# Windowed attention with four adjacent output rows per partition, the value product in two column tiles, and the last unit in one store

## The chip, the cores and the metric

The kernel runs on one core of a Trainium2 chip. The metric is the device time in microseconds (us) of one execution. The span of a profile is some 1.8 us shorter than the time of the same execution (before: 940.6 us and 942.39 us).

## The reference, cut to what matters

```python
B, S, D, W = 4, 4096, 1536, 64              # float32 in and out
q_w, k_w, v_w = (x.reshape(B, S // W, W, D) for x in (q, k, v))
logits = einsum('bnwd,bnud->bnwu', q_w, k_w) * D ** -0.5
attn   = softmax(logits)                    # over the 64 keys of the window
out    = einsum('bnwu,bnud->bnwd', attn, v_w).reshape(B, S, D)
```

There are 16384 rows; each window of 64 rows attends only to itself. The program reads 302 MB and writes 101 MB, and computes little.

## The kernel before

It works through 32 units of 512 rows. GpSimd issues all loads but the first of q (cast to fp16 on the way, two units ahead, two landing buffers per tensor) and all stores but the last, and copies each landed tensor into the working buffer. TensorE transposes q and k, forms logits, and multiplies the exponentials with v; VectorE and ScalarE copy transposes and scale the output by the reciprocal of the row sums.

```python
# [cut] P=128 partitions, SLOTS=4 rows per partition and unit, R=2, H=2, NO=3 output buffers
def rows(x, row0, n, r):     # r adjacent rows lie in one partition
    return x[row0 : row0 + P * n].rearrange("(h p r) d -> p h (r d)", p=P, r=r)

def store(u):                # two adjacent rows: 256 runs of 12288 B
    nc.gpsimd.dma_start(
        out=rows(of, u * UR, SLOTS, R), in_=slots(outs[u % NO], 0, SLOTS, R)
    ).then_inc(d_o[u % NO], 16)

def hand_over(x, u, dst, m, g):
    gp.wait_ge(landed[x][u % NL], 16 * ((u + u % NL) // NL))
    gp.wait_ge(m, u)
    gp.tensor_copy(out=dst..., in_=landing[x][u % NL]...).then_inc(c_l, 1)
    # [cut: wait for the copy, tell TensorE]
    request(x, u + NL)       # the load of two units later

# TensorE, value product: one weight set for all 128 output rows of a row slot
for h in range(H):
    for t, r, what in ((1,0,"s"), (1,1,"s"), (0,0,"sv"), (0,1,"sv"), (1,0,"v"), (1,1,"v")):
        n = R * h + t
        w = ets[h][:, r, t, :]                       # 128 x 128
        ld = nc.tensor.ldweights(w)
        # [cut] "s": the row sums; "v": three matmuls of 512 columns of v16[:, R*h + r, :]

# GpSimd's loop
for u in range(1, N):
    hand_over("q", u, q16, m_q, g_q)
    hand_over("k", u, k16, m_k, g_k)
    gp.wait_ge(m_q, u + 1)
    store(u - 1)
    hand_over("v", u, v16, m_v, g_v)

# SyncE, the last unit in two stores
for h, c in enumerate((1, 3)):
    for a in range(2):
        sy.wait_ge(n_e[a], c)
    sy.dma_start(out=rows(of, base + R*P*h, R, R), in_=slots(o, R*h, R*h + R, R)).then_inc(d_l[h], 16)
```

The softmax here doesn't subtract the row's maximum and nothing guards it: scores larger than these inputs give would overflow.

## Time and profile before

| | before |
|---|---|
| time, median of the first 3 runs | 942.81 us (942.58 to 943.32) |
| span of the profiled run | 940.6 us |
| late unit | 29.17 us |
| early unit, inputs prefetched | 20.4 us |
| granted TensorE clock | 0.86 |

The slices of the page show the busy share of each engine in tenths. A full DMA row beside a TensorE row of 6 to 8 says that transfers bound the kernel. The lines are in the prediction.

The trace has one record for every DMA packet (start, duration, bytes, queue), without the number of the DMA engine that carried it. Each DMA ends with one 4-byte completion packet on each of the 16 engines. Sorting the 16 completion packets of one DMA gives when the first engine and the last engine were done with it; the difference is called the **spread**. One engine is followed by taking, at the end of a packet, the packet that starts there; where several start together this can slip, so such chains are used only where one engine is clearly apart from the others.

### The profile page before, as it was taken

The page shows a single profiled execution, that of the slowest core. Times are in us where ns is not written, and L with a number is a line of the kernel's source. Part 1 is how long each engine was busy: PE and PEld are TensorE (multiplying, and loading weights), DVE is VectorE, ACT ScalarE, POOL GpSimd, SP SyncE. Part 2 cuts the span into 40 slices and gives each one's busy share as a digit, 9 for nine tenths or more (in the row PEclk, how much of TensorE's full clock was granted, in tenths as well). Part 3 has the DMA queues.
Part 4 walks back from the last instruction along what each step waited for, and adds up shares of the span by engine and source line. Part 5 has one row for each costly group of instructions (what it writes and reads, how often), then busy time and mean ns, then how long its engine had stood idle before and what let it go on. Part 6 is the DMA issues. An engine that isn't in the chain of part 4 may idle for free. (4 is left out here: it accounts for less than half of the span.)

```text
span 940.6 us, 11415 instructions
## 1 busy us (share of the span) xinstructions
PE 656.9 (70%) x4096; PEld 397.2 (42%) x3456; DVE 279.9 (30%) x453; ACT 335.6 (36%) x642; POOL 341.0 (36%) x225
## 2 busy tenths in 40 slices
PE   0888676866777768677676676776867768677673
PEld 0555344533445434454244443445433445334450
DVE  0344322333313333133331333321333223332231
ACT  0444433333333333332432324332334333343332
POOL 4244333344333443333423334233343333433221
PEclk9999978889878788888887978887789788888887
DMA  9999999999999999999999999999999999999998
GB/s 258 218 217 274 259 241 283 283 280 268 233 283 283 279 276 230 277 284 279 281 232 271 283 280 283 238 263 283 280 282 247 253 283 281 282 255 245 283 297 367
DMA packets 26652, 253.35 MB, mean 269 GB/s; under 512 B 2064, under 2 KB 2064, under 8 KB 10256
## 3 DMA queue, kind: packets, MB, share of 16 engines
q0 software_dynamic: 26208, 246.95, 100.0%
q1 hardware_dynamic: 432, 6.29, 1.6%
q14 instruction: 10, 0.08, 0.0%
q8 instruction: 2, 0.03, 0.0%
HBM read 301.99 MB, written 100.66 MB: 428 GB/s over the span
## 5 line engine op out<-in xcount | busy, mean ns | idle before, releaser
L155 PE MATMUL lt<-xq,xk 128*128 128x256 f16 x1536 | 215.5, 292 | 0.0
L143 PE MATMUL tp<-ident,k 128*128 128x128 f32 x768 | 146.9, 335 | 82.9 <-PEq L209 71.7
L292 POOL COPY v<-vl 128x3072 f32<-128x3072 f32 x31 | 85.1, 2744 | 287.4 <-DMA vl<-in_v_dram 287.4
L155 PEld LDWEIGHTS lt<-xq,xk 128*128 128x128 f16 x1536 | 159.5, 104 | 32.8
L143 PE MATMUL tp<-ident,q 128*128 128x128 f32 x768 | 113.9, 297 | 75.4 <-PEq L209 39.3
L143 PEld LDWEIGHTS tp<-ident,k 128*128 128x128 f32 x768 | 113.9, 174 | 102.8 <-issue 100.2
L218 ACT COPY xk<-tp 128x512 f32<-128x512 f32 x96 | 59.3, 618 | 260.1 <-ACTq L209 260.1
L184 PEld LDWEIGHTS <-et 128*128 128x128 f16 x384 | 34.6, 108 | 277.9 <-issue 272.2
L143 PEld LDWEIGHTS tp<-ident,q 128*128 128x128 f32 x768 | 92.7, 152 | 115.9 <-issue 115.2
L218 DVE COPY xk<-tp 128x512 f32<-128x512 f32 x96 | 66.5, 693 | 225.9 <-DVEq L209 225.9
L292 POOL COPY k<-kl 128x3072 f32<-128x3072 f32 x31 | 85.3, 2750 | 109.2 <-DMA kl<-in_k_dram 109.2
L292 POOL COPY q<-ql 128x3072 f32<-128x3072 f32 x31 | 85.1, 2744 | 106.3 <-DMA ql<-in_q_dram 106.3
L111 PE MATMUL o<-v,et 128*128 128x512 f16 x384 | 114.4, 443 | 0.0
L218 ACT COPY xq<-tp 128x512 f32<-128x512 f32 x96 | 59.7, 622 | 130.9 <-ACTq L209 130.9
L260 ACT ACTIVATE et<-lt,zeros 32x128 f16<-32x128 f32 x256 | 92.1, 360 | 39.3 <-ACTq L209 36.1
L111 PE MATMUL sp<-ones,et 128*128 128x1 f16 x256 | 25.6, 169 | 112.3 <-PEq L209 110.0
L247 DVE TENSOR_SCALAR out<-o,rs 128x512 f32<-128x512 f32 x128 | 91.1, 747 | 34.1 <-DVEq L209 29.9
L218 DVE COPY xq<-tp 128x512 f32<-128x512 f32 x96 | 66.2, 690 | 97.8 <-DVEq L209 97.6
L271 ACT ACTIVATE out<-tp,rs 128x512 f32<-128x512 f32 x64 | 44.0, 688 | 134.6 <-ACTq L209 104.4
L111 PE MATMUL tp<-v,et 128*128 128x512 f16 x256 | 91.1, 443 | 0.0
L237 DVE RECIPROCAL rs<-sp 128x2 f32<-128x2 f32 x64 | 10.7, 168 | 259.5 <-DVEq L209 259.3
L111 PE MATMUL lt<-v,et 128*128 128x512 f16 x128 | 57.6, 450 | 0.0
(21 smaller groups left out, 224.5 us busy)
## 6 DMA issues: line engine op xcount, KB each, us to landing
out_dram<-out POOLq DMA_DIRECT2D x31, 3072.0 KB, 61.7
ql<-in_q_dram POOLq DMA_DIRECT2D x31, 1536.0 KB, 54.9
kl<-in_k_dram POOLq DMA_DIRECT2D x31, 1536.0 KB, 54.9
vl<-in_v_dram POOLq DMA_DIRECT2D x31, 1536.0 KB, 54.9
out<-in_q_dram SPq DMA_DIRECT2D x1, 3072.0 KB, 16.8
out_dram<-out SPq DMA_DIRECT2D x2, 1536.0 KB, 9.5
k<-in_k_dram POOLq DMA_DIRECT2D x1, 1536.0 KB, 18.0
v<-in_v_dram POOLq DMA_DIRECT2D x1, 1536.0 KB, 24.3
```

The lines of the kernel that those rows point to most:

```text
L111: return nc.tensor.add_instruction(mybir.InstMatmult(name=nc.get_next_instruction_name(), engine=PE, ins=[low(rhs), low(w)], outs=[low(o)] ...
L143: ins = nc.tensor.transpose(tps[g % 2][:, r, j, :], pairs[:, c * P : (c + 1) * P], ident[:, :])
L155: ins = nc.tensor.matmul(lts[h][:, r, :, :], lhsT=halves(xk, c)[:, r, h, :, w], rhs=halves(xq, c)[:, :, h, :, w], start=(c == 0 and w == 0 ...
L184: ld = nc.tensor.ldweights(w)
L218: copy(out=dst, in_=tps[g % 2][:, :, :, :]).then_inc(f_c[g % 4], 1)
L237: ve.reciprocal(out=rs[:, n : n + R], in_=sp[:, n : n + R]).then_inc(n_d, 1)
L247: ins = ve.tensor_scalar_mul(scaled(u, n, j), bank(n, j), scalar1=rs[:, n : n + 1])
L260: ins = sc.activation(ets[h][s, :, :, s], lts[h][s, :, :, s], EXP, bias=zeros[s, 0:1], scale=scale)
L271: ins = sc.activation(scaled(u, n, j), bank(n, j), COPY, bias=0.0, scale=rs[:, n : n + 1])
L292: gp.tensor_copy(out=dst[:, :, :].bitcast(FP32), in_=landing[x][u % NL][:, :, :].bitcast(FP32)).then_inc(c_l, 1)
```

## The change

The output of a unit is to lie with four adjacent rows in each partition, so that a store has 128 runs of 24576 B and not 256 of 12288 B. Then the 128 partitions of one row slot come from both halves of the unit (64 from each), and each half has its own v rows. So each row slot is computed by two matmuls, each with 64 weight columns and its own v, which sit beside each other in TensorE as two column tiles. The reciprocal of the row sums is now taken per row slot, and the last unit is stored by one DMA.

```diff
-    ets = [sb(f"et{h}", [P, R, R, P], FP16) for h in range(H)]
+    ets = [sb(f"et{h}", [P, R, SLOTS, P // H], FP16) for h in range(H)]
@@ a matmul of the value product
-                tile_size=(P, P), tile_position=(0, 0),
+                tile_size=(P, P // H), tile_position=(0, P // H * h),
@@ value product (cut)
+        for n in range(SLOTS):
+            for r in range(R):
+                w = [ets[h][:, r, n, :] for h in range(H)]
+                for h in range(H):
+                    ld = nc.tensor.ldweights(w[h], tile_position=(0, P // H * h))
+                    if n == r == 0:
+                        ld._wait_ge(f_x[h], 1)
+                # [cut: two row sums]
                 for j in range(NJ):
+                    for h in range(H):
+                        ins = reuse(h, half(bank(n, j), h), w[h],
+                            v16[:, R * h + r, 512 * j : 512 * (j + 1)], r == 0, r == R - 1)
@@ VectorE
-            if n % R == 0:
-                await_(ve, p_s)
-                ve.reciprocal(out=rs[:, n : n + R], in_=sp[:, n : n + R]).then_inc(n_d, 1)
+            await_(ve, p_s)
+            ve.reciprocal(out=rs[:, n : n + 1], in_=sp[:, n : n + 1]).then_inc(n_d, 1)
@@ store
-            out=rows(of, u * UR, SLOTS, R), in_=slots(outs[u % NO], 0, SLOTS, R)
+            out=rows(of, u * UR, SLOTS, SLOTS), in_=slots(outs[u % NO], 0, SLOTS, SLOTS)
@@ last unit
-        for h, c in enumerate((1, 3)):
-            for a in range(2):
-                sy.wait_ge(n_e[a], c)
-            sy.dma_start(
-                out=rows(of, base + R * P * h, R, R), in_=slots(o, R * h, R * h + R, R)
-            ).then_inc(d_l[h], 16)
+        for a in range(2):
+            sy.wait_ge(n_e[a], 3)
+        sy.dma_start(
+            out=rows(of, (N - 1) * UR, SLOTS, SLOTS), in_=slots(outs[(N - 1) % NO], 0, SLOTS, SLOTS)
+        ).then_inc(d_l, 16)
```

The rest of the diff follows from these: index orders of the transposed q and of the exponentials, and the semaphores of the new order.

More of the change, by code (lines that the diff above doesn't have):

```diff
@@ L66 @@
     zeros = sb("zeros", [P, 4], FP32)
-    ets = [sb(f"et{h}", [P, R, R, P], FP16) for h in range(H)]
+    ets = [sb(f"et{h}", [P, R, SLOTS, P // H], FP16) for h in range(H)]
     rs = sb("rs", [P, 4], FP32)
     tps = [ps(f"tp{i}", [P, R, H, P]) for i in range(2)]
-    lts = [ps(f"lt{h}", [P, R, R, P]) for h in range(H)]
+    lts = [ps(f"lt{h}", [P, R, SLOTS, P // H]) for h in range(H)]
     ops = [ps(f"o{j}", [P, 512]) for j in range(NJ)]
@@ L76 @@
     d_o = [sem(f"d_o{i}") for i in range(NO)]
-    d_l = [sem(f"d_l{i}") for i in range(2)]
+    d_l = sem("d_l")
     g_q, g_k, g_v = (sem(n) for n in ("g_q", "g_k", "g_v"))
@@ L83 @@
     p_l, p_s = sem("p_l"), sem("p_s")
+    f_s = [sem(f"f_s{n}") for n in range(SLOTS)]
     p_o = [sem("p_od"), sem("p_oa")]
@@ L106, in load, with reuse @@
         ).then_inc(s, 16)
-    def reuse(o, w, rhs, start, stop):
+    def reuse(h, o, w, rhs, start, stop):
         low = nc.tensor.lower_ap
@@ L122, in take, with keys, queries, half @@
         return ins._wait_ge(s, 1)
-    def halves(xt, c):
-        return xt[:, c, :].bitcast(FP16).rearrange("p (r h e w) -> p r h e w", r=R, h=H, w=2)
+    def keys(c, h, r, w):
+        k = xk[:, c, :].bitcast(FP16).rearrange("p (r h e w) -> p r h e w", r=R, h=H, w=2)
+        return k[:, r, h, :, w]
+    def queries(c, h, w):
+        k = xq[:, c, :].bitcast(FP16).rearrange("p (s h e w) -> p s h e w", s=SLOTS, h=H, w=2)
+        return k[:, :, h, :, w]
+    def half(t, h):
+        return t[P // H * h : P // H * (h + 1)]
     def bank(n, j):
@@ L156, in product @@
                         lts[h][:, r, :, :],
-                        lhsT=halves(xk, c)[:, r, h, :, w],
-                        rhs=halves(xq, c)[:, :, h, :, w],
+                        lhsT=keys(c, h, r, w),
+                        rhs=queries(c, h, w),
                         start=(c == 0 and w == 0 and r == 0),
@@ L177, in tensor_unit @@
         await_(nc.tensor, g_v)
-        for h in range(H):
-            for t, r, what in (
-                (1, 0, "s"), (1, 1, "s"), (0, 0, "sv"), (0, 1, "sv"), (1, 0, "v"), (1, 1, "v")
-            ):
-                n = R * h + t
-                w = ets[h][:, r, t, :]
-                ld = nc.tensor.ldweights(w)
-                if what == "s" and r == 0:
-                    ld._wait_ge(f_x[h], 1)
-                if "s" in what:
-                    ins = reuse(sp[:, n : n + 1], w, ones[:, 0:1], r == 0, r == R - 1)
-                    if t == 0 and r == R - 1:
-                        ins.then_inc(p_s, 1)
-                    elif t == 1 and r == R - 1:
-                        ins.then_inc(f_x[h], -1)
-                    elif t == 1 and h == 1:
-                        ins._wait_ge(f_o[0][0], 1).then_inc(f_o[0][0], -1)
-                if "v" not in what:
-                    continue
-                for j in range(NJ):
-                    ins = reuse(
-                        bank(n, j), w, v16[:, R * h + r, 512 * j : 512 * (j + 1)], r == 0, r == R - 1
-                    )
-                    if r == R - 1:
-                        ins.then_inc(p_o[on_act(n, j)], 1)
-                    elif n and (n, j) != (2, 0):
-                        s = f_o[j][(n - 2) % 4]
-                        ins._wait_ge(s, 1).then_inc(s, -1)
@@ new lines, in tensor_unit @@
+        for n in range(SLOTS):
[6 more added lines that the diff above has]
+                for h in range(H):
+                    ins = reuse(h, half(sp, h)[:, n : n + 1], w[h], ones[:, 0:1], r == 0, r == R - 1)
+                    if r == 0 and h == 0:
+                        s = f_s[(n - 1) % SLOTS]
+                        ins._wait_ge(s, 1).then_inc(s, -1)
+                    elif h == H - 1 and r == R - 1:
+                        ins.then_inc(p_s, 1)
+                    elif n == SLOTS - 1:
+                        ins.then_inc(f_x[r], -1)
+                for j in range(NJ):
+                    for h in range(H):
+                        ins = reuse(
+                            h, half(bank(n, j), h), w[h],
+                            v16[:, R * h + r, 512 * j : 512 * (j + 1)], r == 0, r == R - 1,
+                        )
+                        if r == R - 1 and h == H - 1:
+                            ins.then_inc(p_o[on_act(n, j)], 1)
+                        elif r == h == 0 and n:
+                            s = f_o[j][(n - 2) % 4]
+                            ins._wait_ge(s, 1).then_inc(s, -1)
@@ L216, in copy_out @@
             eng.sem_inc(m_q if g < DC else m_k, 1)
-        dst = xt[:, g % DC, :].rearrange("p (r e j) -> p r j e", r=R, j=H)
+        order = "p (j r e) -> p r j e" if g < DC else "p (r e j) -> p r j e"
+        dst = xt[:, g % DC, :].rearrange(order, r=R, j=H)
         copy(out=dst, in_=tps[g % 2][:, :, :, :]).then_inc(f_c[g % 4], 1)
     def scaled(u, n, j):
-        h, t = n // R, n % R
-        return outs[u % NO][:, R * h + t, 512 * j : 512 * (j + 1)]
+        return outs[u % NO][:, n, 512 * j : 512 * (j + 1)]
     def told(ins, u, n, j, a):
@@ L234, in vector_unit @@
         for n in range(H * R):
-            if n % R == 0:
-                await_(ve, p_s)
-                ve.reciprocal(out=rs[:, n : n + R], in_=sp[:, n : n + R]).then_inc(n_d, 1)
-                await_(ve, n_d)
-                ve.sem_inc(n_r, 1)
+            await_(ve, p_s)
+            ve.reciprocal(out=rs[:, n : n + 1], in_=sp[:, n : n + 1]).then_inc(n_d, 1)
+            await_(ve, n_d)
+            ve.sem_inc(f_s[n], 1)
+            ve.sem_inc(n_r, 1)
             if n == 0:
@@ L257, in scalar_unit @@
             await_(sc, p_l)
-            for a in range(0, P, W // R):
-                s = slice(a, a + W // R)
+            for a in range(P * R // W):
+                s, t = (slice(a * W // r, (a + 1) * W // r) for r in (R, SLOTS))
                 ins = sc.activation(
-                    ets[h][s, :, :, s], lts[h][s, :, :, s], EXP, bias=zeros[s, 0:1], scale=scale
+                    ets[h][s, :, :, t], lts[h][s, :, :, t], EXP, bias=zeros[s, 0:1], scale=scale
                 )
@@ L265, in scalar_unit @@
         for n in range(H * R):
-            if n % R == 0:
-                await_(sc, n_r)
+            await_(sc, n_r)
             for j in range(NJ):
@@ L341 @@
             sy.sem_inc(fr[a], NO)
+        sy.sem_inc(f_s[-1], 1)
         sy.wait_ge(i_p, 1)
@@ L359 @@
             hand_over("v", u, v16, m_v, g_v)
-        base, o = (N - 1) * UR, outs[(N - 1) % NO]
-        for h, c in enumerate((1, 3)):
-            for a in range(2):
-                sy.wait_ge(n_e[a], c)
-            sy.dma_start(
-                out=rows(of, base + R * P * h, R, R), in_=slots(o, R * h, R * h + R, R)
-            ).then_inc(d_l[h], 16)
+        for a in range(2):
[3 more added lines that the diff above has]
+        ).then_inc(d_l, 16)
         gp.drain()
@@ L374 @@
             sy.wait_ge(d_o[i], 16 * (last // NO + 1))
-        for i in range(2):
-            sy.wait_ge(d_l[i], 16)
+        sy.wait_ge(d_l, 16)
         lo, hi = min(s.num for s in sems), max(s.num for s in sems)
```

## The prediction

> **What bounds the kernel now.** I read the page's slices first, then the DMA part, then the waits, then windows over whole units, and last the tail in the timeline. The kernel works through 32 units of 512 rows: transpose q and k on TensorE, form logits, exponentiate, multiply with v, scale on two engines, store.
>
> The slices and the queue lines of the page:
>
> ```profile
> PE   0888676866777768677676676776867768677673
> DMA  9999999999999999999999999999999999999998
> DMA packets 26652, 253.35 MB, mean 269 GB/s; under 512 B 2064, under 2 KB 2064, under 8 KB 10256
> ...
> q0 software_dynamic: 26208, 246.95, 100.0%
> q1 hardware_dynamic: 432, 6.29, 1.6%
> ...
> HBM read 301.99 MB, written 100.66 MB: 428 GB/s over the span
> ...
> out_dram<-out POOLq DMA_DIRECT2D x31, 3072.0 KB, 61.7
> ```
>
> Every DMA slice is full while PE is at 6 to 8 tenths. The GB/s of the slices understate the traffic, because loads are cast and counted by the fp16 bytes that they write; the HBM line has both directions. A store takes 61.7 us from issue to landing, far longer than its own 3 MB needs, so it stands in a queue.
>
> Windows over two early and two late units, each from one first q transpose to the next (columns: length, busy time and count of PE, PEld, DVE, ACT, POOL, granted clock, DMA share, GB/s):
>
> ```profile
> 44.88:65.28 20.40, 17.00 (x129) 10.78 (x108) 8.62 (x15) 10.36 (x21) 9.89 (x7) 1.00 1.03 216
> 65.28:85.70 20.42, 17.01 (x129) 10.79 (x108) 8.63 (x15) 10.34 (x21) 8.82 (x7) 1.00 1.02 232
> 577.76:606.93 29.17, 21.58 (x129) 12.98 (x109) 7.80 (x13) 9.97 (x20) 10.77 (x7) 0.82 1.02 270
> 606.93:636.09 29.16, 19.86 (x128) 12.72 (x109) 9.54 (x16) 10.82 (x21) 10.77 (x7) 0.88 1.02 270
> ```
>
> This is the main evidence. With data prefetched, compute does a unit in 20.4 us; once the prefetched units are used up, a unit takes 29.17 us, at the same DMA share of 1.02. So some 8.8 us of a unit are slack of compute, and the larger PE time of the late units is the lower clock (0.82 to 0.88) that goes with waiting.
>
> The waits say on what:
>
> ```profile
> POOL v L292 <- DMA vl<-in_v_dram: 287.4, 29, 10.5
> ...
> PE sp L111 <- PEq L209: 110.0, 29, 4.5
> ```
>
> GpSimd waits for v in 29 units, some 10 us each; TensorE waits at the head of the value product in the same 29.
>
> The trace's packet records give the DMA bound exactly. Following one engine from packet to packet, start to start: a 24576 B packet of q or k takes 907.0 ns, a 12288 B packet of v 455.3 ns, a 12288 B store packet 456.5 ns, without gaps. A unit gives each engine 8 packets of q, 8 of k, 16 of v, 16 of the store: 16 x 907.0 + 16 x 455.3 + 16 x 456.5 = 29101 ns, plus four short completion packets of some 10 ns: 29.14 us, against 29.17 measured.
>
> The tail:
>
> ```profile
> 917.38 2.74 POOL L292 COPY v<-vl 128x3072 f32<-128x3072 f32 x1 [10.47 <-DMA vl<-in_v_dram]
> ...
> 920.32 0.21 PE L111 MATMUL sp<-ones,et 128*128 128x1 f16 x3 [4.12 <-PEq L209]
> ...
> 927.19 1.83 SPq L366 DMA_DIRECT2D out_dram<-out  x2
> 927.25 1.41 DVE L247 TENSOR_SCALAR out<-o,rs 128x512 f32<-128x512 f32 x2
> ```
>
> The last v lands at 917.4, the last scaling ends at 928.66, the last data packet on the DMA engines at 939.0. In between the engines are not idle: by the packet records two earlier stores are still in their queues, which the 16 engines finish between about 929 and 932 us (the engines have drifted apart); then each does its 16 packets of the last store, 16 x 456.5 = 7.3 us. So even the end is DMA time.
>
> **What the Trainium skill says.** "DMA: Bandwidth & Descriptors", section "Where 436 GB/s comes from": the fabric ceiling is 435.2 GB/s. The trace agrees: 24576 B in 907.0 ns on 16 engines is 433.5 GB/s, 12288 B in 456.5 ns is 430.7. Same page, "Why small descriptors are slow (HBM only)": a packet has a small fixed cost of about 3 cycles. The trace agrees in kind: 2 x 455.3 - 907.0 = 3.6 ns for one more packet. Same page, "Issuing engines are not separate DMA queues": transfers from several engines interleave on the same 16 DMA engines; agreed, the last stores issued by SyncE follow the GpSimd stores on the same engines. "TensorE: Matmul & The Clock Gate", part 3 ("Packing small matmuls — row/col tiling"): column tiles run concurrently, 2.38x for three; no run yet shows it here.
>
> **The change part by part.**
>
> Stores. A partition's output becomes four adjacent rows, one run of 24576 B instead of two of 12288 B: 128 data packets for 256 per unit. Bytes are the same, and the engines already move them at 99% of the ceiling. Fixed cost: a 12288 B read at 455.3 ns with 3.6 ns fixed is 451.7 ns of pure movement; a store packet at 456.5 then has 4.8 ns fixed. I estimate the large store packet at 2 x 451.7 + 4.8 = 908.2 ns, against 913.0 for two: 4.8 ns saved per pair, 8 pairs per engine and unit, 32 units: 1.23 us. This lies on the bounding resource, so it counts in full. If the 3.6 ns hold for stores also, 0.92 us; if the cost goes with bytes, 0.
>
> TensorE, value product. Per unit, 24 matmuls of 128x512 become 48 of 64 columns by 512, the 8 row sums 16, the 12 weight loads 16. If two column tiles stream together, the time is that of 24: with the clock warm the product takes 5.55 us a unit (units 0 to 2), 7.2 us in most others. New: each of the four row-slot groups waits for the reciprocal of the one before. Working it from the timeline: group 2 would start about 1.4 us after group 1's last matmul began, and VectorE has two scalings of group 1 (1.41 us) ahead of the reciprocal (0.17 us): a stall of 0.1 to 0.4 us, at most four times, so up to 1 us a unit. The first weight load now needs both exponentials instead of the first one, some 1.5 us; in the late units both are done before v is copied (918.4 against 920.1 in the last unit). All this lies in the 8.8 us of slack; v's request is issued some 55 us ahead of its landing, so DMA does not starve. On the path: nothing, except in the last unit.
>
> VectorE gets 4 reciprocals for 2, 2 x 0.17 = 0.34 us a unit, in slack (it is 30% busy). ScalarE keeps 8 exponentials of 32 partitions x 128. GpSimd issues a store with half the runs: 0.715 us should fall towards the 0.55 us of the one-run loads, in slack.
>
> Tail. One store after all scaling, instead of the first half at 927.2 and the second at about 928.7. The last v lands some 1.1 us earlier through the stores; the last product takes 0.2 to 0.8 us longer. The one store is issued at about 928.4. The first half's packets began some 1.7 us after its issue, so packets are there from about 930.1, while the slowest engine leaves its queued stores at about 930.8 (932 less 1.2). That engine sets the end, so it loses nothing; if compute is slower than I think, it loses up to 1 us. I take 0.2 us.
>
> Sum: 942.81 - 1.2 + 0.2 = 941.8 us.
>
> **Rivals.**
>
> The two halves do not overlap on TensorE. Then 24 passes of 213 ns at full clock (the trace: 640 ns for three) are added, 5.1 us a unit: 20.4 becomes 25.5 us, still under 29.17. So even this fails to become the bound, unless the clock stays low; only the tail pays, 5 to 7 us less 2 us of slack: about 945 to 947. Against it: the skill's measured column packing.
>
> TensorE becomes the bound by waits and mode changes on top of serial halves. It needs 8.8 us more per unit; with 5.1 from serial halves, 3.7 us from drains and reciprocals would have to come. Then 2 to 5% slower. Little speaks for it.
>
> Longer runs help HBM itself, beyond packet cost. The ceiling speaks against it: with the movement itself unchanged, removing every fixed cost (48 packets of about 4 ns per engine and unit, 0.2 us) gives 0.7%, 6 us: 936.5 at the very best. So faster by 2% (924 us) is out of reach.
>
> The store's saving is nil and the late single store leaves a gap: 943 to 944.5.
>
> **Range and chances.** The centre is 941.8; nil saving and a gap give the upper edge 944.2, a somewhat larger gain the lower edge 940.2. Faster by 2% 0.01, within 2% 0.96, slower 0.03 (the second rival).
>
> **What would show it.** Right: 22556 packets in all (4096 fewer), the store packets near 908 ns apart, DMA slices still full, late units of 29.13 us, the waits for v still about 10 us in 29 units, TensorE's early units about 1 to 2.5 us longer than 20.4. Serial halves would show as a value product of 11 us or more in the early units. Wrong: units whose length follows TensorE, with GpSimd no longer waiting for v; or store packets whose pitch is clearly under 904 ns, which the byte rate forbids; or idle DMA engines before the last store.

## The result, and the profile after

The changed kernel took **942.99 us** (median of 6 runs, 942.77 to 943.88), the kernel before 942.77 us (6 runs, 942.58 to 943.32). The ratio is 1.0003 (95% interval 0.9990 to 1.0016): the same. Ratios here are the mean time of one kernel's fast runs over that of the other's of the same rounds, so not quite the ratio of the medians quoted. The profiled execution of before was one of its shortest (942.39 us, span 940.6) and that of after took 943.07 us (span 941.3); a comparison of the two traces therefore explains 0.7 us, where the medians differ by 0.2.

Slices, queues and issues of the page of the changed kernel:

```profile
PE   0877777666767767768676586676866767757673
DMA  9999999999999999999999999999999999999997
DMA packets 22540, 253.35 MB, mean 269 GB/s; under 512 B 2048, under 2 KB 2048, under 8 KB 10240
...
q0 software_dynamic: 22240, 246.95, 99.7%
...
HBM read 301.99 MB, written 100.66 MB: 428 GB/s over the span
...
out_dram<-out POOLq DMA_DIRECT2D x31, 3072.0 KB, 61.6
```

There are 4112 packets fewer and every DMA slice but the last is still full: the bound is the same. Windows over two early and two late units of the changed kernel (columns as in the prediction):

```profile
48.43:71.85 23.42, 17.89 (x162) 10.93 (x112) 8.96 (x16) 10.45 (x20) 10.58 (x7) 1.00 1.03 216
71.85:95.27 23.42, 17.89 (x162) 10.94 (x112) 8.96 (x16) 10.44 (x20) 10.58 (x7) 1.00 1.01 279
577.60:607.06 29.46, 19.77 (x162) 11.07 (x112) 8.96 (x16) 10.46 (x20) 10.75 (x8) 0.88 1.02 270
607.06:635.74 28.68, 20.63 (x162) 11.99 (x112) 8.96 (x16) 10.46 (x20) 10.10 (x7) 0.88 1.02 270
```

Early units, which compute sets, are 3.0 us longer (23.42 for 20.40); late ones average 29.07 us in these two windows, again at a DMA share of 1.02. The compute that was added lies in the slack. The waits of the changed kernel:

```profile
POOL v L300 <- DMA vl<-in_v_dram: 278.3, 28, 10.8
...
PE sp L112 <- PEq L218: 130.6, 27, 5.7
...
PE sp L112 <- DVEq L247: 5.3, 18, 0.3
```

GpSimd still waits some 10 us a unit for v. The third line is the wait of TensorE for the new reciprocals (0.3 us each, 5.3 us in the whole run).

The value product at full clock, from the timelines (start, length, engine, what, count): first before, then after.

```profile
61.30 1.46 PE L111 MATMUL o<-v,et 128*128 128x512 f16 x6
```

```profile
66.92 0.84 PE L112 MATMUL o<-v,et 128*64 128x512 f16 x6
```

Six matmuls of 128 columns took 1.46 us; six of 64 columns, as three pairs, 0.84. If the two of a pair came one after the other, the time would be the same as before. The column tiles do run side by side. A whole product grew from 5.55 to 6.59 us in early units.

In the packet records the pitch of a store packet is 908.0 ns, against 2 x 456.5 = 913.0 before, and a late unit on the first engine takes 29.127 us, before 29.165. The first engine leaves the last store that GpSimd queued at 927.85 us instead of 929.11: **1.26 us earlier. The engine that ends last did not gain this**, and it sets the end. The tail, in windows of 2 us (columns as above; the last two are the DMA share and GB/s), before and after:

```profile
928.00:930.00 2.00, 0.00 (x0) 0.00 (x0) 0.67 (x2) 0.26 (x1) 0.00 (x0) 1.00 1.00 424
930.00:932.00 2.00, 0.00 (x0) 0.00 (x0) 0.00 (x0) 0.00 (x0) 0.00 (x0) 0.69 1.04 442
```

```profile
928.00:930.00 2.00, 0.00 (x0) 0.00 (x0) 1.21 (x2) 0.49 (x1) 0.00 (x0) 1.00 0.29 123
930.00:932.00 2.00, 0.00 (x0) 0.00 (x0) 0.00 (x0) 0.00 (x0) 0.00 (x0) 0.85 1.12 455
```

and the timeline of the last unit of the changed kernel:

```profile
917.14 2.75 POOL L300 COPY v<-vl 128x3072 f32<-128x3072 f32 x1 [10.78 <-DMA vl<-in_v_dram]
...
920.20 0.19 PE L112 MATMUL sp<-ones,et 128*64 128x1 f16 x2 [4.05 <-PEq L218]
...
927.80 1.41 DVE L256 TENSOR_SCALAR out<-o,rs 128x512 f32<-128x512 f32 x2 [0.45 <-DVEq L218]
...
929.24 0.35 SPq L373 DMA_DIRECT2D out_dram<-out  x1
```

The copy of the last v began only 0.24 us earlier than before (917.14 for 917.38), since it waits for the last of the 16 engines: in the changed kernel the first was done with v at 913.29, the last at 916.72. Most engines ran dry from 928 to 930, until the packets of the last store came at 930.08. That hole looks like the loss, but the engine that ends last had work until 931.6. Its account, in us of the span:

| on the engine that ends last | before | after |
|---|---|---|
| first engine done with the DMA ahead of the last queued store | 921.80 | 920.58 |
| + spread at that DMA | 2.53 | 3.48 |
| + two stores at their pitch (32 x 0.4565; 16 x 0.908) | 14.61 | 14.53 |
| + packets over their pitch | 0 | 0.29 + 0.58 |
| sum | 938.94 | 939.46 |
| measured end of data | 938.95 | 939.47 |

So a gain of 1.22 us is met by 0.95 us of spread and 0.87 us of slow packets. The 0.29 us are in the last queued store; its eight packets on that engine, in ns (nominal 912 of duration, at a pitch of 908):

```
967  973  973  987  935  916  912  928
```

The 0.58 us are a fetch of instructions of 8192 B, 309 ns, at 933.43 us, which fell on this engine, and a packet after it of 1180 ns instead of 912. Before, such a fetch came at 932.50, on an engine that did not end last.

The two columns are not about the same engine. In the kernel before, one engine stood 2.53 us behind the first from early on and ended last. Another fell back slowly, by slow packets in its stores: from 0.67 us behind at 149 us to 1.39 at the DMA ahead of the last queued store. In the changed kernel such an engine fell back from 0.62 us to 3.48. It passed the others, of which the latest stood at 2.52, at about 730 us, and ended last. In both traces the late fetch of instructions falls on the engine that falls back, so it is probably the same one; the trace has no engine numbers to prove it. Had it kept its place, the end would have been near 920.58 + 2.52 + 14.53 = 937.6 us, 1.3 us under the kernel before (an estimate from the table).

### The profile page after: what moved, and what is told of

It reads as the page before. It is cut to its first block, busy times and chain, and to the rows that moved or that the text cites. A ratio compares the mean times of both kernels' runs of the same rounds, so it can differ in the third digit from the quotient of the medians.

```text
span 941.3 us, 13141 instructions
## 1 busy us (share of the span) xinstructions
PE 641.9 (68%) x5120; PEld 371.9 (40%) x3584; DVE 288.4 (31%) x517; ACT 336.0 (36%) x642; POOL 334.1 (35%) x225
## 2 busy tenths in 40 slices
DMA packets 22540, 253.35 MB, mean 269 GB/s; under 512 B 2048, under 2 KB 2048, under 8 KB 10240
## 5 line engine op out<-in xcount | busy, mean ns | idle before, releaser
L164 PE MATMUL lt<-xq,xk 128*128 128x256 f16 x1536 | 203.3, 282 | 0.0
L192 PEld LDWEIGHTS <-et 128*64 128x64 f16 x512 | 40.5, 131 | 331.6 <-issue 319.4
L152 PE MATMUL tp<-ident,k 128*128 128x128 f32 x768 | 124.9, 297 | 57.9 <-PEq L218 40.5
L112 PE MATMUL sp<-ones,et 128*64 128x1 f16 x512 | 52.6, 178 | 147.8 <-PEq L218 130.6
L152 PEld LDWEIGHTS tp<-ident,q 128*128 128x128 f32 x768 | 85.9, 145 | 120.8 <-issue 120.7
L152 PEld LDWEIGHTS tp<-ident,k 128*128 128x128 f32 x768 | 96.0, 152 | 75.1 <-issue 73.1
L245 DVE RECIPROCAL rs<-sp 128x1 f32<-128x1 f32 x128 | 21.4, 167 | 323.8 <-DVEq L218 323.2
L112 PE MATMUL o<-v,et 128*64 128x512 f16 x768 | 117.7, 440 | 0.0
L112 PE MATMUL tp<-v,et 128*64 128x512 f16 x512 | 100.2, 468 | 0.0
L112 PE MATMUL lt<-v,et 128*64 128x512 f16 x256 | 64.5, 479 | 0.0
```

What stands on the lines that cost most here:

```text
L112: return nc.tensor.add_instruction(mybir.InstMatmult(name=nc.get_next_instruction_name(), engine=PE, ins=[low(rhs), low(w)], outs=[low(o)] ...
L152: ins = nc.tensor.transpose(tps[g % 2][:, r, j, :], pairs[:, c * P : (c + 1) * P], ident[:, :])
L164: ins = nc.tensor.matmul(lts[h][:, r, :, :], lhsT=keys(c, h, r, w), rhs=queries(c, h, w), start=(c == 0 and w == 0 and r == 0), stop=(c == ...
L192: ld = nc.tensor.ldweights(w[h], tile_position=(0, P // H * h))
L245: ve.reciprocal(out=rs[:, n : n + 1], in_=sp[:, n : n + 1]).then_inc(n_d, 1)
```

## The experiments

Twelve kernels ran; all gave correct results. The kernel before: 942.92, 942.66, 942.98 and 942.7 us median. The theory at first: the 1.2 us were saved on every engine and the hole ahead of the single last store gave them back. The rivals: the saving reaches 15 engines of 16 only and the last one alone sets the end; nothing was saved at all; the two column tiles run in turn, or change mode slowly.

**1. The changed kernel with the last unit in two stores again**

```diff
-        for a in range(2):
-            sy.wait_ge(n_e[a], 3)
-        sy.dma_start(out=rows(...), in_=slots(...)).then_inc(d_l, 16)
+        for h, c in enumerate((1, 3)):
+            for a in range(2):
+                sy.wait_ge(n_e[a], c)
+            sy.dma_start(
+                out=last_rows[:, R * h : R * h + R, :],
+                in_=outs[(N - 1) % NO][:, R * h : R * h + R, :],
+            ).then_inc(d_l[h], 16)
```

> The changed kernel, with the last unit's output stored in two halves again (slots 0 and 1 as soon as they are scaled, then slots 2 and 3), each of 12288 B runs. My theory: the changed kernel saves 1.2 us of DMA time in its stores and loses most of it again at the end, because the one last store is issued at 929.2 us, when most of the 16 DMA engines have run dry since about 928. Then this run starts its last stores by about 927.4, shows no idle engines between 928 and 930, and takes 0.7 to 1.2 us less than the changed kernel: 941.8 to 942.3 us, also 0.5 to 1.0 us under the kernel before. Rival A, the larger store packets save nothing over a whole run (other delays of the slowest engine eat it): the time stays at 942.7 to 943.1 us, that of the kernel before. Rival B, the end is set by the slowest engine alone, whatever the time of issue: no change against the changed kernel, 943.0 us.

Measured: 942.88 us (942.87 to 944.28), ratio 1.0004 (0.9990 to 1.0017). The tail windows of this run:

```profile
928.00:930.00 2.00, 0.57 (x6) 0.00 (x0) 1.47 (x3) 1.07 (x2) 0.00 (x0) 1.00 0.78 320
930.00:932.00 2.00, 0.00 (x0) 0.00 (x0) 0.11 (x1) 0.00 (x0) 0.00 (x0) 1.00 0.92 387
```

The hole is mostly filled (0.78 for 0.29), the packets come at 928.75 instead of 930.08, and the time has not moved. My first theory fell: the idle stretch of the other engines cost nothing. This is rival B. The last engine left the queued store at 931.87 (931.61 in the changed kernel), and the same fetch, 309 ns and 0.27 us after it, fell on it again.

**2. The kernel before with the last unit in one store**

```diff
-        for h, c in enumerate((1, 3)): ...
+        for a in range(2):
+            sy.wait_ge(n_e[a], 3)
+        sy.dma_start(
+            out=rows(of, (N - 1) * UR, SLOTS, R), in_=slots(outs[(N - 1) % NO], 0, SLOTS, R)
+        ).then_inc(d_l, 16)
```

> The kernel before, with its last unit in one store after all scaling; nothing else. My theory: issue moves from 927.2 and 928.7 us to about 928.9 us, its first packets to about 930.6; the engines of the kernel before leave their queued stores between 929 and 932 us, so some engines idle for up to 1.5 us and the slowest not at all: 0.2 to 0.8 us slower than the kernel before, 943.0 to 943.6 us. Rival B (only the slowest engine counts): no change, 942.8 us. A rival that says a late single store costs its whole delay: 1.5 us, 944.3 us.

Measured: 943.35 us (943.02 to 943.60), 0.4 us over the kernel before, in the expected range, but not clear of noise (ratio 1.0003, 0.9990 to 1.0017), and the profiled run gives another reason than my theory. There the DMA ahead of the last queued store had a first engine at 922.06 and a spread of 3.10; with two stores of 14.61 us in all that makes 939.77, and the data ended at 939.78. So all that this run lost on the profiled run before (938.95) was lost ahead of the last stores, and the single store by itself cost nothing that the trace shows.

**3. The changed kernel with the column tiles in turn**

```diff
-                for j in range(NJ):
-                    for h in range(H):
+                for h in range(H):
+                    for j in range(NJ):
```

> The changed kernel, with the order of the value product's matmuls changed so that the two column tiles do not alternate: three matmuls of the one half, then three of the other. Same instructions, same waits. My theory: alternating halves stream at once; apart, only the last of one half and the first of the other can overlap, so five to six passes of 213 ns instead of three per weight set: the product of an early unit (6.59 us in the changed kernel) takes 9.8 to 12 us, the early units 27 to 29 us instead of 23.4, and the total still is that of the changed kernel plus the last unit's longer product (2 to 5 us): 945 to 948 us, while the late units stay at 29.1 us. Rival C, the halves never overlapped in the changed kernel: the product takes 6.6 us here as well, and the time stays at 943.0 us. Rival D, TensorE has no slack: late units grow to 31 us or more, the total to 1000 us.

Measured: 944.15 us (943.76 to 944.41, 4 runs), ratio 1.0011 (0.9996 to 1.0027). Two early units:

```profile
48.10:73.05 24.95, 19.55 (x161) 11.60 (x113) 8.96 (x16) 10.44 (x20) 10.59 (x7) 0.93 1.02 215
73.05:98.19 25.14, 19.89 (x161) 11.43 (x113) 8.96 (x16) 10.43 (x20) 10.58 (x7) 0.93 1.02 276
```

These units are 1.5 to 1.7 us longer than in the changed kernel, and their products took 8.13 and 8.31 us against 6.59. But most of this is not the order. The granted clock is 0.93 here and 1.00 there: a stretch of half clock lay in each of the two products. Windows over it and over a later product of this run at full clock (same columns):

```profile
66.32:69.73 3.41, 3.41 (x23) 0.70 (x4) 1.17 (x3) 1.51 (x3) 0.53 (x1) 0.50 1.14 238
115.08:122.24 7.16, 7.12 (x65) 1.46 (x17) 3.49 (x8) 3.22 (x5) 3.20 (x2) 1.00 1.00 361
```

All four products of this run at full clock took 7.09 to 7.28 us, all four of the changed kernel 6.59. So the order costs 0.5 to 0.7 us a product, and I had expected 3.2 us or more. The first two weight sets of that product show why:

```profile
115.11 0.61 PE L112 MATMUL tp<-v,et 128*64 128x512 f16 x4
115.54 0.40 PE L112 MATMUL lt<-v,et 128*64 128x512 f16 x2
115.76 0.19 PE L112 MATMUL sp<-ones,et 128*64 128x1 f16 x2
```

The six matmuls of a set take 0.65 us from the first start to the next set, as in the changed kernel (65.36 to 66.01). The single records of the second set, in us, with the half to which each belongs (the second half is known by the semaphores that it increments):

```
115.785 first  115.809 second  116.000 first  116.024 second  116.215 first  116.239 second
```

In the program all three of the first half come ahead of all three of the second. Yet the second half starts 24 ns after the first and streams beside it. So the tiles overlap in this order too. The Trainium skill, "TensorE: Matmul & The Clock Gate", part 3, "The mechanism", has matmuls start and end strictly in program order; the starts recorded here do not agree. Thus the run does not serve as the control that it was meant to be. That the tiles overlap in the changed kernel rests on the timelines shown above (0.84 us for 1.46) and on its single records, where the two of a pair start 23 to 31 ns apart. Late units stayed at 29.13 us on the first engine. The 1.2 us come in the tail: the spread ahead of the last queued store was 4.27 us for 3.48, and the last store, issued at 931.88 instead of 929.24, began its packets at 932.73, when the latest engine had been done since 932.50.

**4. The changed kernel with each store as two DMAs of 12288 B runs**

```diff
     def store(u):
-        nc.gpsimd.dma_start(
-            out=rows(of, u * UR, SLOTS, SLOTS), in_=slots(outs[u % NO], 0, SLOTS, SLOTS)
-        ).then_inc(d_o[u % NO], 16)
+        four = of[u * UR : (u + 1) * UR].rearrange("(p r) d -> p r d", p=P)
+        for h in range(2):
+            nc.gpsimd.dma_start(
+                out=four[:, R * h : R * h + R, :],
+                in_=outs[u % NO][:, R * h : R * h + R, :],
+            ).then_inc(d_o[u % NO], 16)
```

(and the waits for a store count 32 instead of 16).

> The changed kernel, with each unit's store but the last cut into two DMAs of slots 0, 1 and slots 2, 3: 256 packets of 12288 B a unit again, as in the kernel before; compute and the last store as in the changed kernel. My theory: store packets 456.5 ns apart, 16 per engine and unit, 7304 ns instead of 8 x 908.0 = 7264: 40 ns a unit, 31 units, 1.2 us, and 0.3 us for one more completion packet per engine and unit; of this 1.5 us up to 0.8 us hides in the gap in front of the last store: 0.7 to 1.5 us slower than the changed kernel, 943.7 to 944.5 us. Rival A (packet size of the stores is worth nothing): 943.0 us.

Measured: 945.43 us (944.96 to 945.84), ratio 1.0025 (1.0011 to 1.0038), over the expected range. A unit on the first engine took 29.171 us for 29.127. These 0.044 us are about what 8 pairs of packets at 5.0 ns and one more completion packet come to, and bring the first engine back to 929.42. The saving by large packets is real. The other half of the loss is again the latest engine: it left at 934.19, 4.77 us behind the first, where the changed kernel has 3.76. It fell back from 1.05 us at 120 us to 4.46 at 907, so it does this with 12288 B packets too.

**5. The changed kernel, the store issued when the next v has landed**

The slow packets of the latest engine lie after the end of a GpSimd copy, about when GpSimd issues the next request. So the next question was whether GpSimd's issuing causes them.

```diff
             gp.wait_ge(m_q, u + 1)
+            gp.wait_ge(landed["v"][u % NL], 16 * ((u + u % NL) // NL))
             store(u - 1)
```

> The changed kernel, with GpSimd issuing each unit's store only when the next v has landed, about 11 us later than now, at the same place in the queue. In the traces of the changed kernel and of the first two runs made from it, one DMA engine loses 0.05 to 0.17 us in nearly every large store, in packets that begin within 1 us before to 3 us after GpSimd's issue of the next k load and of the next store; that engine ends 3.8 us behind the first one and sets the end. Theory: the loss comes with GpSimd's issuing while a store is being read. Then with the store's issue out of that stretch (0.54 us of issuing left of 1.26) the spread of the engines at the end falls from 3.8 us to about 2.7 us and the total to 942.2 to 942.7 us. Rival: the loss belongs to the large packets or to the new compute, not to the issue: spread 3.8 us, total 943.0 us as in the changed kernel.

Measured: 944.92 us (944.86 to 945.37), ratio 1.0025 (1.0011 to 1.0039). Missed: the spread grew instead, to 4.50. Two effects add up here, since the last store also came late (issued at 932.20, in the changed kernel 929.24):

```profile
930.00:932.00 2.00, 0.63 (x6) 0.00 (x0) 1.41 (x3) 1.13 (x2) 0.00 (x0) 1.00 0.06 25
```

Here the DMA engines, the latest aside, were really empty, and the end moved from 939.47 to 941.11. Of these 1.64 us, 1.06 are the latest engine, which left the queue at 932.67 instead of 931.61. Then it stood idle too: the packets of the last store came at 933.04 at the earliest. This is what a hole that costs looks like: it outlasts the latest engine, here by some 0.4 us.

**6 and 8. The store placed behind the request for v, in the changed kernel and in the kernel before**

```diff
             hand_over("k", u, k16, m_k, g_k)
+            hand_over("v", u, v16, m_v, g_v)
             gp.wait_ge(m_q, u + 1)
             store(u - 1)
-            hand_over("v", u, v16, m_v, g_v)
```

> The changed kernel, with each unit's store placed after the v load in GpSimd's order instead of before it; nothing else. Then the last v lands one store (7.3 us) earlier in the queue, and three stores instead of two lie behind it while the last unit is computed. Theory: the gap before the last store goes away (the engines have work until about 929 to 932 us, the last store is issued at about 922 us), so nothing is left but the stream of the slowest engine: 0.3 to 1.0 us under the changed kernel, 942.0 to 942.7 us. Rival, the end is set by the slowest engine alone and the gap costs nothing: 943.0 us. Rival, the buffers of the output come free too late (their slack of some 10 us shrinks by 7): late units longer than 29.15 us, total over 944 us.

> The kernel before, with the store after the v load as in the previous run but one. It shows what the change itself is worth when neither of the two has a gap in front of its last store. Theory: the kernel before has no such gap, so the order alone moves it little: 942.6 to 943.0 us; the changed kernel with the same order is then 0.3 to 1.0 us faster than this. Rival (the larger packets of the store are worth nothing at the end): both equal within 0.2 us.

Measured: 945.96 us (945.78 to 946.12) for the changed kernel, 948.74 us (947.77 to 948.93) for the kernel before, both far over what was expected. In both, one engine lost about 0.2 us in each store. The third forecast, output buffers that come free too late, is not the reason: a unit on the first engine took 29.127 and 29.165 us, as without the new order. The second result is the more telling one: with 12288 B packets and the old value product the same drift appears. So it needs neither the large packets nor the column tiles; the place of the store in the queue alone can bring it. (In run 8 the data ended 3.85 us later than in the kernel before, and the span was 6.4 us longer; the other 2.5 us, after the last packet, are not explained.)

**7. The changed kernel with stores in runs of 3072 B**

```diff
+                out=four[:, :, D // 2 * h : D // 2 * (h + 1)],
+                in_=outs[u % NO][:, :, D // 2 * h : D // 2 * (h + 1)],
```

> Made from the run with two stores a unit (945.4 us), with the two DMAs split by columns instead of by rows: 1024 packets of 3072 B a unit instead of 256 of 12288 B. Theory of a fixed cost per packet: a packet takes 3072/12288 x 451.7 + 4.8 = 117.7 ns, 64 of them 7534 ns per engine and unit instead of 16 x 456.5 = 7304: 0.23 us a unit, 31 units, 7.1 us: 952.5 us. Rival, the cost goes with bytes: 945.4 us.

Measured: 949.69 us (949.54 to 950.09, 4 runs), ratio 1.0073. The page of this run counts

```profile
DMA packets 34941, 253.36 MB, mean 267 GB/s; under 512 B 2544, under 2 KB 2544, under 8 KB 26608
```

that is some 7900 more than with two stores of 12288 B. Four times as many store packets would be 23800 more. The trace records the stores in 15872 packets of 6144 B, two runs to a packet, so my sum counted too many. On the first engine a unit grew by 0.08 us, for 16 packets more: 5.0 ns each, near the 4.8 that I had taken. On the median engine it grew by 0.18 us, which the number of packets does not explain. So the cost per packet is there on the first engine, and the 4.3 us of the whole run are more than that.

**9, 10 and 11. Nothing issued by GpSimd during a store**

The k request, the store and the v request are issued together after the copy of v; 9 is the changed kernel, 10 the same with two last stores, 11 the kernel before.

```diff
-            hand_over("k", u, k16, m_k, g_k)
+            hand_over("k", u, k16, m_k, g_k, ask=False)
+            hand_over("v", u, v16, m_v, g_v, ask=False)
+            request("k", u + NL)
             gp.wait_ge(m_q, u + 1)
             store(u - 1)
-            hand_over("v", u, v16, m_v, g_v)
+            request("v", u + NL)
```

> The changed kernel, with GpSimd issuing the next k load and the store together with the next v load, after the copy of v; the order of the queue (q, k, store, v) is unchanged, all three are issued while the DMA engines run a q load, and GpSimd issues nothing while they run a store. TensorE's work on k still starts during each store, as before. Theory I (the engine that loses time in each store loses it to GpSimd's issuing): no slow store packets any more, the spread of the engines in the last queued store falls from 3.8 us to the 2.0 to 2.6 us that they have after 100 us, the last v lands 1 us earlier, and the total is 941.6 to 942.4 us. Theory II (it loses it to the work of TensorE, VectorE and ScalarE on k, which begins during the store): spread 3.5 to 5 us and total 943.0 to 945 us, as in the runs so far.

> The previous run with the last unit stored in two halves. If theory I holds, this takes away both losses of the changed kernel: no drift, and a first half in the queue before the engines run dry (issued at about 926.5 us): 941.3 to 942.0 us, the best of all and 0.8 to 1.5 us under the kernel before. If theory II holds: 942.9 us or more, no better than the kernel before.

> The kernel before, with the same shift of GpSimd's issues. Its slowest engine in the last queued store is one that was late from the start, so there is less to win: theory I: drift of 0.8 us gone but off the path, 942.3 to 942.9 us. The difference to the previous run is then what the larger store packets are worth, predicted 1.2 us. Theory II: 942.8 us, unchanged.

Measured: 943.15 (942.77 to 944.13), 943.05 (942.77 to 943.25) and 942.93 us (942.46 to 943.04); ratios 1.0005, 1.0001 and 0.9999. GpSimd's part of the timeline of 9, from 812 to 826 us, holds one line:

```profile
814.65 2.75 POOL L300 COPY k<-kl 128x3072 f32<-128x3072 f32 x1 [3.41 <-DMA kl<-in_k_dram]
```

Nothing is issued there, and yet the spread grew to 3.46, as in the changed kernel (3.48). GpSimd's issuing is not the cause: theory I fell, and run 10 missed its 941.3 to 942.0 us. Run 9 lies where theory II put it (943.0 to 945 us; the spread at the lower edge of 3.5 to 5).

**12. As 10, with a useless second GpSimd copy after that of k**

```diff
             hand_over("k", u, k16, m_k, g_k, ask=False)
+            gp.tensor_copy(
+                out=landing["k"][u % NL][:, :, :].bitcast(FP32), in_=k16[:, :, :].bitcast(FP32)
+            ).then_inc(c_l, 1)
+            copies[0] += 1
+            gp.wait_ge(c_l, copies[0])
```

> The run before last (quiet stores, last unit in two halves), with GpSimd copying k once more, from its buffer back to the buffer in which it landed, right after its copy of k: useless work of 2.75 us that nobody waits for. In all traces so far the slow packets of the one engine begin when GpSimd's copy of k (or of v, where the store was placed behind v) ends, whatever TensorE does at that time. Theory: the loss belongs to what follows the end of that copy on GpSimd; then with the second copy the slow stretch begins some 3 us later, when nearly all of the store is over, the drift of 2.9 us falls under 1 us, the spread in the last queued store from 3.1 to 2.0 to 2.7 us, and the total to 942.0 to 942.7 us. Rival (the work on k that the end of the first copy releases): the slow packets stay where they are, drift 2.5 to 3.5 us, total 942.9 to 943.3 us.

Measured: 943.46 us (942.70 to 943.87), ratio 1.0009 (0.9995 to 1.0023). The two copies in the timeline:

```profile
814.60 2.75 POOL L300 COPY k<-kl 128x3072 f32<-128x3072 f32 x1 [3.42 <-DMA kl<-in_k_dram]
817.51 2.75 POOL L367 COPY kl<-k 128x3072 f32<-128x3072 f32 x1 [0.16 <-POOL k L300]
```

If the slow packets came with GpSimd falling idle, they would move behind the second copy. They stayed: 82% of their time lies under it. This theory fell as well. They still follow the end of the first copy, which hands k to TensorE, as the rival said; the median time lies above what either expected. The profiled run happened to be the fastest of the five (942.70 us). Its spread stayed at 2.88, but the engine that loses time fell back as elsewhere, from 0.55 to 2.86 us, and had just drawn level.

**The spread over the run.** The table has the spread in us at five of the 126 DMAs that GpSimd issued (four a unit, counted from 0), in the kernels where it is most instructive:

| DMA number | 24 | 56 | 88 | 104 | 124 |
|---|---|---|---|---|---|
| before | 2.53 | 2.53 | 2.53 | 2.53 | 2.53 |
| after | 2.37 | 2.48 | 2.52 | 2.72 | 3.48 |
| 1, last in two | 2.45 | 2.79 | 2.79 | 2.79 | 3.17 |
| 5, store late | 2.25 | 2.30 | 3.07 | 3.73 | 4.50 |
| 6, store after v | 2.38 | 2.73 | 4.30 | 5.07 | 6.45 |
| 8, before, store after v | 2.70 | 2.85 | 3.93 | 4.73 | 6.39 |
| 12, second copy | 2.27 | 2.88 | 2.88 | 2.88 | 2.88 |

The second latest engine never got beyond 2.92 in these runs; it is one engine that drifts off. Its slow packets are the last of a store. In the changed kernel 77 of 3429 store packets between 130 and 905 us took over 16 ns more than nominal, 3.07 us together; before 18 of 6814, 0.58 us. Packets of v were never slowed.

A spread that stays flat does not mean that this engine loses nothing. Followed by its slow packets from store to store, it falls back all through the run: in the changed kernel 0.62 us behind the first at 149 us, 1.38 at 411, 2.51 at 702, 3.48 at DMA 124. The spread grows only after it has passed all others. In run 1 it passed the latest only at about 790 us, in run 12 it had just reached it at the end (2.86).

How much it loses goes with the kernel. In the old order of the queue it fell back by less than 1 us in the kernel before and in runs 2 and 11, which have the old product, and by 2.3 to 3.8 us in the changed kernel and in runs 1, 3, 4, 5, 9, 10 and 12, which have the new one; run 4 has the packet size of the kernel before. So the compute side of the change, or the timing that it brings, raised the loss. Run 8 shows that the new product is not needed for it.

**Why that engine loses time stays open.** It does not need the large packets (4, 8). Ruled out are GpSimd's issuing (9) and GpSimd's falling idle after its copy (12). Standing, and not tested by a run of its own, is the rival of runs 9 and 12: the work of TensorE, VectorE and ScalarE that the end of a copy releases while the store is being read.

No version beat both kernels: the best, 1, 10 and 11, are level with before.

## Why the prediction was right or wrong, point by point

The range held; the point lay 1.2 us below the measured 943.0. That the range held is partly luck: its upper part stood for no saving or a gap, and what came was a saving that another engine ate.

- **Bound by DMA throughout: right.** The slices stayed full, and GpSimd waited for v 28 times, some 10 us each (29 predicted).
- **Saving per pair of store packets, 4.8 ns: right.** The pitch is 908.0 ns (predicted 908.2; so 5.0 ns saved), a late unit on the first and the median engine 29.127 us (predicted 29.13). Runs 4 and 7 confirm it from the other side.
- **Packets: nearly.** 22540, not 22556; one last store fewer also spares 16 completion packets.
- **Column tiles run at once: right**, by the timeline. Early units are 3.0 us longer, over my 1 to 2.5. Of this the product is 1.04 us, the start that waits for both exponentials 1.55 us (from 0.75 to 2.3 us between the last logit matmul and the product), the q transposes 0.3.
- **All of it in slack: right.** GpSimd's issue of a store fell from 0.715 to 0.538 us (about 0.55 predicted), also in slack.
- **The second rival** (TensorE becomes the bound) did not come, nor did serial halves. In run 3 even early units of 25 us, lengthened by a stretch of half clock, left late units at 29.13 us on the first engine.
- **The tail: the step that failed.** The prediction said "the slowest engine leaves its queued stores at about 930.8 (932 less 1.2)". It left at 931.6, and the end was held up by another 0.58 us. The sum took the saving of most engines for that of all, and took for granted that the engine which was slowest before stays so. Another engine, 1.39 us behind in the kernel before and 3.48 in the changed one, passed it. The first engine did gain 1.26 us, and the last gained nothing: the spread of 3.48 for 2.53 and the slow packets (0.95 + 0.87 us in the profiled runs) outweigh the 1.22 saved. The term "-1.2" was right for most engines and wrong for the one that sets the end. That the hole before the last store is harmless ("That engine sets the end, so it loses nothing") was right, and my first theory after the result wrongly dropped it; run 1 brought it back.

## What to carry to other kernels

When a kernel is bound by DMA at 99% of what its engines move, merging packets that are already 12 KB saves some 5 ns a pair: count it before reworking a product for it. A saving per packet counts only if the latest of the 16 engines gets it, so look at the completion packets of the first and of the last engine, not at a mean pitch, and follow an engine that loses time even while it is not the last. An idle stretch of most engines ahead of the last transfer costs nothing while one engine is still busy with the queue. Compare the time of a product only between stretches of the same granted clock: run 3 would have passed for a proof otherwise.

## What the Trainium skill lacked or had wrong

- "DMA: Bandwidth & Descriptors", section "Why small descriptors are slow (HBM only)", calls merging worthwhile only for descriptors of 256 B or less. As a rule of thumb that held: going from 12288 to 24576 B saved 5.0 ns a pair, 1.26 us of 942 on the first engine and nothing in the time. But the page has no measured figure for middle sizes; stores recorded in packets of 6144 B instead of 12288 B cost 4.3 us of 945 here, 5.0 ns a packet on the first engine and more on others.
- The same page, section "Latency and other measured facts", says that DMA engines 7 and 15 are usually slower and gives a best guess for the cause. The trace has no engine numbers, so no run here shows which engine it is. What the page lacks: the 16 engines stood 2.5 us apart in a kernel of 942 us, and one engine could drift off by 0.2 us a store to 6.4 us of spread, by slow packets of stores, depending on the order of the queue and on the compute beside it (0.7 us in the kernel before, 2.9 us in the changed one).
- "TensorE: Matmul & The Clock Gate", part 3, has a measured figure for three column tiles of 32 columns, none for two of 64. Here six matmuls of 64 columns by 512 took 0.84 us as three pairs, where six of 128 columns took 1.46 us. Its statement that matmuls start strictly in program order does not hold for the starts in the trace of run 3: with three matmuls of one tile ahead of three of the other in the program, the two tiles still started 24 ns apart, and a product took 7.09 to 7.28 us instead of 6.59 at full clock.
- "Runtime: NRT & Kernel Launch", section "Instruction fetch mechanics", tells of instruction fetches as something that the fetching engine can wait for, not of what they cost other transfers. Here a fetch of 8192 B took 309 ns on a DMA engine in the tail and the store packet after it 268 ns longer than nominal: 0.58 us at the end, when it falls on the engine that ends last.
